# Hybrid decoder layer on one core: the feed-forward's down projection by one level of Strassen's form

## The chip, the cores and the metric

The kernel runs on one core of one Trainium2 chip. The metric is device time in microseconds (us) of one execution, the median of the runs shown; less is better. The matrix engine TensorE is called PE here, VectorE DVE, ScalarE ACT, GpSimd POOL, and the queue of SyncE, which issues all transfers named below, SP. L1056 is line 1056 of the kernel before, unless the text says that it is of the changed kernel.

## The reference

One layer for 2048 tokens of width 1024: a mixer (two groups of attention heads) with residual and LayerNorm, then a gated feed-forward network with a causal depthwise convolution of width 3 on the gate, again with residual and LayerNorm. The change lies in the feed-forward network alone:

```python
def conv_glu_ffn(h, w_ff_gate, w_ff_up, conv_w, conv_b, w_down):   # D_FF = 2816
    gate = h @ w_ff_gate
    up = h @ w_ff_up
    gp = jnp.pad(gate, ((0, 0), (CONV_WIDTH - 1, 0), (0, 0)))
    conv = sum(gp[:, i:i + S, :] * conv_w[i] for i in range(CONV_WIDTH)) + conv_b
    return (jax.nn.silu(conv) * up) @ w_down
# in the layer:
    y = conv_glu_ffn(h, ...)
    x = layer_norm(DEEPNORM_ALPHA * x + (1.0 + gate_f) * y, ln2_g[l], ln2_b[l])
```

## The kernel before

Everything is float32. A product is made of three passes of TensorE over operands that are split into a high and a low part (high by high, high by low, low by high). ACT makes the high part by a copy, DVE or POOL the low part by a subtraction; L101 is the line of a helper through which these urgent splits are issued, on each of the three engines.

**Gate and up.** The 2048 tokens are four tiles of 512, taken in two pairs, t2 = 0 and 1. The 22 blocks of 128 features are taken in 11 feature pairs, fp. For each t2 and fp there are two units, one for the gate and one for the up projection (unit, L1035). A unit makes two feature blocks for two token tiles by one level of Strassen's form: seven products of 12 matmuls of 128x512. For that the four quarters of the unit's weights are summed on DVE (tile wsum) and split (w_hi by ACT, w_lo by POOL for pieces of 128x1024, by DVE for those of 128x512). The sums of the token tiles are made once for each t2 (store_sums, L950; POOL's additions on tiles k, L958 to 961) and stored in DRAM. The first two feature pairs of the first two token tiles are done without Strassen's form (plain, L1108).

The gate unit's result goes through the convolution on DVE (conv_silu, L1103 to 1105) and SiLU on ACT (L1106) into a tile cv of 128x1024, one for each of the two feature blocks; there are two such buffers in all. The up unit multiplies its results into cv: put (L1051) adds the pieces on DVE into a small tile k (L1055; a ring of six buffers), POOL multiplies k into cv (L1056). Then cv is stored to the DRAM tensor da (L1090), and its buffer is free for the next pair's convolution.

**Down.** The activations (2048 x 2816) times w_down (2816 x 1024) are made in two halves of 512 output columns. Each half goes over 16 blocks of 128 tokens; a block is one accumulation over 22 feature blocks, three passes each (row_wide, L419 to 421). load_a (L1176) fetches a block's activations from da in three parts and splits them, in buffers that gate and up used before (pl, gt, wsum, cv in turn). The weights of the first half are loaded (L1162) and split while the last units run. In the first half the gated rows with their residual are stored to DRAM (dr0, L1224), in the second they come back (L1211), and DVE ends each block: gating, residual and statistics (L1217 to 1219), then the norm (L385 to 395), before the output is stored.

The order on each engine is set by a scheduler that simulates a timeline; what is issued through the urgent helper goes ahead of the rest. Each engine then runs its own list in order and waits at the head of it.

Of the kernel before, what the change touches and what calls it, by code (L numbers as in the profile page):

```python
# [27 lines left out]
P = 128  # L29
# [56 lines left out]
def layer(tc, x, c, w_ada, b_ada, w_in, gla_w_gate, gla_b_gate, sb_norm_g, gla_norm_g, w_out,  # L86
# [347 lines left out]
    da = [dram.tile([P, 2 * NB, NFF, P], F32, name=f"da{t}") for t in range(NT2)]  # L434
    dsum = {(t, i): [dram.tile([P, TQ], F32, name=f"dsum{t}{i}_{k}") for k in range(4)]
            for t in range(NT2) for i in (1, 3, 4, 6)}
    dr0 = [dram.tile([P, 512], F32, name=f"dr0_{b}") for b in range(NT * NB)]
# [400 lines left out]
    def run(gen):  # L838
        for _ in gen:
            pass  # L840
# [194 lines left out]
    def unit(n, order=range(7), after={}):  # L1035
# [25 lines left out]
        for i in order:  # L1061
# [35 lines left out]
            if i in after:  # L1097
                after[i]()

# [8 lines left out]
    def plain(t, x):  # L1108

        xh, xl = ([w[:, i, :] for half in x for w in half] for i in range(2))  # L1110
        for fp in range(CL):
            wg, wu = (weights(w[:, 256 * fp:256 * (fp + 1)], dve) for w in (w_ff_gate, w_ff_up))
            for j in range(2):
# [12 lines left out]
                nc.sync.dma_start(da[t // 2][:, t % 2 * NB:(t % 2 + 1) * NB, fb, :], cv.rearrange("p (b c) -> p b c", c=P))  # L1126
# [29 lines left out]

    slots = [(i, k) for i in range(7) for k in range(4)]

    def load_down(half, i, dst):

        raw = wring.tile([P, 1024], F32, name="w_raw", bufs=3)
        nc.sync.dma_start(raw.rearrange("p (k c) -> p k c", c=512),  # L1162
                          w_down[256 * i:256 * (i + 1), 512 * half:512 * (half + 1)].rearrange("(k p) c -> p k c", p=P))
        act.copy(dst[0], raw)
        dve.tensor_sub(dst[1], raw, dst[0])
        return [x.rearrange("p (k c) -> p k c", c=512) for x in dst]

    def t_pair(i):
        return [t_tile(*slots[2 * i + j]).rearrange("p k c -> p (k c)") for j in range(2)]

    wd = [[], []]
    for n in range(first, len(units)):
        unit(n, (0, 1, 3, 4, 2, 5, 6) if n == first else range(7))
    n_a = [0]

    def load_a(b):  # L1176

        hi, lo = [], []
        for f0 in range(0, NFF, 8):
            n = min(8, NFF - f0)  # L1180
# [4 lines left out]
            nc.sync.dma_start(w.bitcast(F32), da[b // (2 * NB)][:, b % (2 * NB), f0:f0 + n])  # L1185
# [6 lines left out]
    ahead = [load_a(0)]  # L1192
    wd[0] += [load_down(0, i, t_pair(i)) for i in range(NFF // 2)]
    gfb, g2b, b2b = rows = [t_tile(*slots[22 + i]).rearrange("p k c -> p (k c)").bitcast(F32) for i in range(3)]
    for d, src in zip(rows, (dgate[1], ln2_g, ln2_b)):
        nc.sync.dma_start(d, src.to_broadcast([P, D]))
    for half in range(2):
        ds = slice(half * 512, (half + 1) * 512)
        for b in range(NT * NB):
            xh, xl = ahead.pop()  # L1200
            if b + 1 < NT * NB or half == 0:
                ahead.append(load_a((b + 1) % (NT * NB)))
            ps = psm.tile([P, TQ], F32, name="acc", bufs=3)
            row_wide(ps, wd[half], xh, xl, slice(0, P))
            if half == 0 and b + 2 == NT * NB:
                wd[1] += [load_down(1, i, ring_pair()) for i in range(4)]
            if half == 0 and b + 1 == NT * NB:
                wd[1] += [load_down(1, i, t_pair(i - 4)) for i in range(4, NFF // 2)]
            if half:
                r = t_tile(*slots[25 + b % 2]).rearrange("p k c -> p (k c)").bitcast(F32)  # L1210
                nc.sync.dma_start(r[:, 0:512], dr0[b])  # L1211
                rh = r[:, 512:]
            else:
                rh = small()
            x1 = small()
            nc.sync.dma_start(x1, dx1[b // NB][b % NB][:, ds])
            nc.vector.tensor_mul(rh, ps, gfb[:, ds])  # L1217
            nc.vector.scalar_tensor_tensor(rh, x1, ALPHA, rh, ALU.mult, ALU.add)
            nc.vector.bn_stats(st_all[:, b, half, :], rh)
            if half:  # L1220
# [30 lines left out]
```

## Time and profile before

| | |
|---|---|
| runs | 2961.71, 2973.14, 2974.06 us; median 2973.14 |
| the profiled execution | 2961.73 us, of that 2960.0 us span |
| busy over the span | PE 94%, DVE 68%, ACT 37%, POOL 35% |
| second token pair's units, 2060 to 2437 us | PE busy in 373.49 of 377 us |
| down projection | first matmul at 2451.13 us, last at 2949.27 us |

The span is from the first to the last instruction. Matmuls overlap in the engine: one of 128x512 has a duration of 0.39 us in the rows, but the next starts 0.23 us after it. So PE's pace is read from the starts, and its losses from idle time before an instruction and from the granted clock, a share of full speed. The busy times of the other engines are sums of durations, and a duration includes what an operation waits while it runs.

### The profile page before, as it was taken

The numbers are of one execution on the slowest core, as the hardware profiler recorded it, in microseconds if no ns is written. First come the engines' busy times: TensorE is split into PE (matmuls) and PEld (weight loads), VectorE is DVE, ScalarE is ACT, GpSimd is POOL, SyncE is SP. The second block draws the span as 40 slices with busy tenths as digits, with TensorE's granted clock in tenths as the row PEclk, the third lists the DMA queues.
The fourth block names the chain that finished last, engine by engine and source line by source line (L and its number), as shares of the span: only waits on it lengthen the run. The fifth ranks groups of instructions, "written<-read, shape, count | busy, mean of one in ns | idle before, by whom it ended". The sixth has DMA issues, their size and how long they took to land. (4 is left out here: it accounts for less than half of the span.)

```text
span 2960.0 us, 38115 instructions
## 1 busy us (share of the span) xinstructions
PE 2773.9 (94%) x13387; PEld 2238.8 (76%) x13387; DVE 2018.8 (68%) x2841; ACT 1102.4 (37%) x1866; POOL 1035.4 (35%) x1139
## 2 busy tenths in 40 slices
PE   7989999999999998979879999989999998999998
PEld 6867887877788775657657787867888886888887
DVE  6474567578778779798667777686666765335665
ACT  2442244365557556534223332243232233112111
POOL 2450223246344345375463445462333440000000
PEclk9999999989999998989889999999999999999999
DMA  8977775766584445656785444354222236445553
GB/s 314 362 253 254 252 253 188 260 188 221 168 282 150 136 140 172 187 171 227 258 315 168 119 147 160 109 164 121 80 84 82 82 105 226 133 134 181 166 165 114
DMA packets 370424, 539.62 MB, mean 182 GB/s; under 512 B 25182, under 2 KB 224056, under 8 KB 370232
## 3 DMA queue, kind: packets, MB, share of 16 engines
q1 hardware_dynamic: 368504, 530.89, 55.6%
q0 software_dynamic: 1728, 6.29, 0.6%
q8 instruction: 106, 1.74, 0.2%
q14 instruction: 86, 0.70, 0.1%
HBM read 404.82 MB, written 132.26 MB: 181 GB/s over the span
## 5 line engine op out<-in xcount | busy, mean ns | idle before, releaser
L541 DVE TENSOR_TENSOR_SCAN pp<-pp,beta 128x512 f32<-128x512 f32 (+2 forms) x320 | 390.0, 1235 | 59.1 <-POOL beta L534 31.9
L543 POOL TENSOR_TENSOR beta<-beta,pp 128x512 f32<-128x512 f32 (+2 forms) x160 | 206.5, 1291 | 365.0 <-DVE pp L541 301.0
L101 POOL TENSOR_TENSOR w_lo<-wsum,w_hi 128x1024 fp32r<-128x1024 f32 x80 | 207.9, 2599 | 171.4 <-ACT w_hi L101 171.4
L1014 PE MATMUL acc<-t,w_lo 128*128 128x512 f32 x640 | 246.9, 392 | 9.2 <-DVE w_lo L101 9.2
L1012 PE MATMUL acc<-t,w_hi 128*128 128x512 f32 x640 | 250.4, 393 | 4.9 <-ACT k L1070 4.0
L1013 PE MATMUL acc<-t,w_hi 128*128 128x512 f32 x640 | 249.6, 390 | 0.0
L556 DVE TENSOR_TENSOR wl<-wt,wh 128x512 fp32r<-128x512 f32 (+1 forms) x320 | 185.2, 597 | 77.2 <-ACT wh L555 76.5
L555 ACT CAST wh<-wt 128x512 fp32r<-128x512 f32 (+1 forms) x320 | 161.0, 529 | 192.3 <-PE wt L551 182.7
L101 ACT CAST w_hi<-w_raw 128x512 fp32r<-128x512 f32 (+2 forms) x173 | 125.4, 746 | 253.1 <-PE acc L1013 64.8
L529 ACT ACTIVATE pp<-z 128x512 f32<-128x512 f32 (+2 forms) x320 | 173.5, 543 | 112.5 <-PE z L528 65.1
L292 PE MATMUL acc<-hh,w_hi 128*128 128x512 f32 x480 | 196.6, 411 | 3.2 <-DVE st L101 2.3
L551 PE MATMUL wt<-ident,beta 128*128 128x128 f32 x1088 | 189.6, 292 | 8.7 <-DVE beta L543 5.5
L294 PE MATMUL acc<-hh,w_lo 128*128 128x512 f32 x480 | 194.0, 405 | 0.6 <-POOL w_lo L101 0.6
L293 PE MATMUL acc<-hl,w_hi 128*128 128x512 f32 x480 | 192.4, 401 | 0.0
L101 DVE TENSOR_TENSOR w_lo<-w_raw,w_hi 128x512 fp32r<-128x512 f32 (+1 forms) x140 | 142.2, 1038 | 55.6 <-ACT w_hi L101 30.3
L530 ACT ACTIVATE beta<-z 128x512 f32<-128x512 f32 (+2 forms) x320 | 171.5, 542 | 18.4 <-PE wt L551 18.4
L551 PEld LDWEIGHTS wt<-ident,beta 128*128 128x128 f32 x1088 | 143.7, 150 | 41.8 <-DVE beta L543 7.9
L559 PE MATMUL o_ps<-wl,v 128*128 128x512 f32 (+1 forms) x320 | 133.9, 424 | 35.2 <-DVE wl L556 33.0
L527 PE MATMUL z<-k,q 128*128 128x512 f32 (+2 forms) x320 | 139.2, 439 | 11.4 <-ACT beta L530 8.6
L301 PE MATMUL acc<-w_hi,hh 128*128 128x256 f32 (+1 forms) x512 | 147.7, 289 | 1.4 <-ACT w_hi L101 0.7
L1014 PEld LDWEIGHTS acc<-t,w_lo 128*128 128x128 f32 x640 | 120.5, 188 | 37.4 <-DVE w_lo L101 12.2
L302 PE MATMUL acc<-w_lo,hh 128*128 128x256 f32 (+1 forms) x512 | 146.0, 286 | 0.9 <-POOL w_lo L101 0.9
(331 smaller groups left out, 7301.6 us busy)
## 6 DMA issues: line engine op xcount, KB each, us to landing
w_raw<-in_w_ff_gate_dram SPq DMA_DIRECT2D x48, 512.0 KB
w_raw<-in_w_ff_up_dram SPq DMA_DIRECT2D x48, 512.0 KB
k<-dk SPq DMA_DIRECT2D x160, 128.0 KB
v<-dv SPq DMA_DIRECT2D x80, 256.0 KB
da<-cv SPq DMA_DIRECT2D x40, 512.0 KB
w_hi<-dwi_0h SPq DMA_DIRECT2D x39, 512.0 KB
w_lo<-dwi_0l SPq DMA_DIRECT2D x39, 512.0 KB
q<-dq SPq DMA_DIRECT2D x128, 128.0 KB
```

Source lines behind the costliest of these rows:

```text
L101: return f(*args, **kw)
L292: nc.tensor.matmul(ps, hi[:, k % 4, cs], xh[k], start=(k == 0), stop=False)
L293: nc.tensor.matmul(ps, hi[:, k % 4, cs], xl[k], start=False, stop=False)
L294: nc.tensor.matmul(ps, lo[:, k % 4, cs], xh[k], start=False, stop=(k == nk - 1))
L529: nc.scalar.activation(pp[:, 0:n], z[:, 0:n], AF.Sigmoid, scale=-1.0)
L541: nc.vector.tensor_tensor_scan(pp[:, 0:n][:, ::-1], pp[:, 0:n][:, ::-1], beta[:, 0:n], first, ALU.mult, ALU.bypass)
L543: (nc.gpsimd if i in PMU and jt < PMJ else nc.vector).tensor_mul(beta[:, 0:n], beta[:, 0:n], pp[:, 1:n + 1])
L551: pe.transpose(wt[:, i * P:(i + 1) * P], ws[i][:, ks], ident)
L556: nc.vector.tensor_sub(wl[:, cs], wt[:, cs], wh[:, cs])
L1012: nc.tensor.matmul(ps, w[0][:, k, :], t[k][:, 0, :], start=first and k == 0, stop=False, **add)
L1013: nc.tensor.matmul(ps, w[0][:, k, :], t[k][:, 1, :], start=False, stop=False, **add)
L1014: nc.tensor.matmul(ps, w[1][:, k, :], t[k][:, 0, :], start=False, stop=k == 3, **add)
```

## The change

The down projection becomes seven products over pairs of token blocks (128 tokens each, 512 apart), pairs of feature blocks and the two halves of the output columns: 11 feature pairs by three passes for each product and each of eight block pairs. One product is taken for all eight pairs before the next. The quarters of w_down are summed on POOL (weight_sums, stored in dws), those of the activations too (act_sums, stored in dsa): in place on the cv tiles after each up unit, and on reloaded copies for the two feature pairs that plain made (plain_sums). The partial rows of all pairs stay on chip (top and low), and dr0 is gone. Weights go through a ring of 17 tiles, activations are loaded in two parts.

```diff
-                    nc.sync.dma_start(da[t2][:, :, 2 * fp + j, :], dst[j].rearrange("p (b c) -> p b c", c=P))
+                    nc.sync.dma_start(da[t2][:, :, j, fp], dst[j].rearrange("p (b c) -> p b c", c=P))
...
+        if up:
+            act_sums(t2, fp, dst[0][:, A], dst[1][:, A], dst[0][:, B], dst[1][:, B])
+
+    def act_sums(t2, fp, a11, a12, a21, a22):
+
+        nc.gpsimd.tensor_add(a22, a21, a22)
+        nc.gpsimd.tensor_sub(a21, a11, a21)
+        nc.gpsimd.tensor_sub(a11, a22, a11)
+        nc.gpsimd.tensor_sub(a12, a12, a11)
+        for j, x in enumerate((a22, a11, a21, a12)):
+            nc.sync.dma_start(dsa[t2][:, :, j, fp], x.rearrange("p (b c) -> p b c", c=P))
...
+    def weight_sums():
+
+        for k in range(NH):
+            for j, (m, n) in enumerate(((0, 0), (1, 0), (1, 1))):
+                nc.sync.dma_start(dws[k][4 + j], quarter(m, n, k))
+            b11, b12, b21, b22 = q = [small() for _ in range(4)]
+            for n, d in enumerate(q):
+                nc.sync.dma_start(d, quarter(n // 2, n % 2, k))
+            yield
+            nc.gpsimd.tensor_sub(b11, b12, b11)
+            nc.gpsimd.tensor_sub(b12, b22, b12)
+            nc.gpsimd.tensor_sub(b22, b22, b11)
+            nc.gpsimd.tensor_sub(b21, b21, b22)
+            for d, x in zip(dws[k], (b11, b12, b22, b21)):
+                nc.sync.dma_start(d, x)
+            yield
...
+    def plain_sums():
+
+        for fp in range(CL):
+            q = [small() for _ in range(4)]
+            for n, d in enumerate(q):
+                nc.sync.dma_start(d.rearrange("p (b c) -> p b c", c=P),
+                                  da[0][:, n // 2 * NB:(n // 2 + 1) * NB, n % 2, fp])
+            yield
+            act_sums(0, fp, *q)
+            yield
...
+    wsums = chain(plain_sums(), weight_sums())
+    for n in range(first, len(units)):
+        unit(n, (0, 1, 3, 4, 2, 5, 6) if n == first else range(7))
+        if n >= first + 4:
+            for _ in range(2):
+                next(wsums, None)
+    run(wsums)
...
+        for k in range(NH):
+            w = wset[i][k]
+            nc.tensor.matmul(ps, xh[k], w[:, 0, :], start=k == 0, stop=False)
+            nc.tensor.matmul(ps, xh[k], w[:, 1, :], start=False, stop=False)
+            nc.tensor.matmul(ps, xl[k], w[:, 0, :], start=False, stop=k == NH - 1)
...
+        if i == 0:
+            nc.scalar.copy(r[:, L], ps)
+        elif i == 1:
+            low.append(wide(NW + b))
+            nc.vector.tensor_add(low[b][:, L], r[:, L], ps)
+            nc.scalar.copy(r[:, R], low[b][:, L])
+            gated(r, blk, 0)
+        elif i == 2:
+            nc.vector.tensor_add(low[b][:, L], low[b][:, L], ps)
+        elif i == 3:
+            nc.vector.tensor_add(r[:, R], r[:, R], ps)
+            nc.vector.tensor_add(low[b][:, R], low[b][:, L], ps)
+            gated(low[b], blk + NB, 1)
+            stats(low[b], blk + NB, 1)
+            gated(low[b], blk + NB, 0)
+        elif i == 4:
+            finish(low[b], blk + NB, ps, False)
+        elif i == 5:
+            nc.vector.tensor_add(r[:, R], r[:, R], ps)
+            gated(r, blk, 1)
+            stats(r, blk, 1)
+        else:
+            finish(r, blk, ps, s + 1 == len(steps))
```

Two of the added functions in words: gated multiplies a half row by the gate and adds the residual (two operations of DVE); finish multiplies the product by the gate into a small tile, adds it to the row (L1266 and L1267 of the changed kernel), takes the statistics and runs the norm over the 1024 columns.

**The order on POOL, one feature pair of the second two token tiles.** Before, from the middle of an up unit into the next one: w_lo is the split of weight sums, cv the multiplication by the up results, gt a copy of two columns for the convolution.

```order
L101 TENSOR_TENSOR w_lo<-wsum,w_hi 128x1024
L1056 TENSOR_TENSOR cv<-cv,k_22173 128x512
L101 TENSOR_TENSOR w_lo<-wsum,w_hi 128x1024 x2
L1044 COPY gt<-halo 128x2 x2
L101 TENSOR_TENSOR w_lo<-wsum,w_hi 128x1024
L1056 TENSOR_TENSOR cv<-cv,k_22407 128x512
```

The same place in the changed kernel, with its own line numbers (L102 is the helper, L1057 the multiplication, L1105 to 1108 the four sums of activations, L1192 to 1195 the four sums of weights):

```order
L102 TENSOR_TENSOR w_lo<-wsum,w_hi 128x1024
L1057 TENSOR_TENSOR cv<-cv,k_22272 128x512
L1057 TENSOR_TENSOR cv<-cv,k_22295 128x512
L1192 TENSOR_TENSOR k_22310<-k_22311,k_22310 128x512
L1193 TENSOR_TENSOR k_22311<-k_22313,k_22311 128x512
L1194 TENSOR_TENSOR k_22313<-k_22313,k_22310 128x512
L1195 TENSOR_TENSOR k_22312<-k_22312,k_22313 128x512
L1105 TENSOR_TENSOR cv<-cv 128x512
L102 TENSOR_TENSOR w_lo<-wsum,w_hi 128x1024
L1106 TENSOR_TENSOR cv<-cv 128x512
L102 TENSOR_TENSOR w_lo<-wsum,w_hi 128x1024
L1192 TENSOR_TENSOR k_22468<-k_22469,k_22468 128x512
```

Between the last multiplication of a pair and the next split POOL now has four weight sums and one activation sum, and the other activation sums stand between the splits that the next gate unit waits for.

**The order on DVE, one block's end in the down projection.** Before, in the second half: a split of activations, the block's gating, residual and statistics, and the norm up to its first wide operation.

```order
L101 TENSOR_TENSOR pl<-pl 128x768
L1217 TENSOR_TENSOR t_2_25734<-acc,t_2_22778 128x512
L1218 SCALAR_TENSOR_TENSOR t_2_25734<-k_25736,t_2_25734 128x512
L1219 BN_STATS st<-t_2_25734 128x6
L385 BN_AGGR rn_mv<-st 128x2
L388 TENSOR_SCALAR rn_mv<-rn_mv 128x1
L394 SCALAR_TENSOR_TENSOR t_2_25734<-t_2_25734,rn_mv,t_3_22779 128x1024
```

In the changed kernel, at the begin of the fifth product:

```order
L102 TENSOR_TENSOR pl<-pl 128x768
L1266 TENSOR_TENSOR k_25017<-acc,t_1_23215 128x512
L102 TENSOR_TENSOR gt<-gt 128x640
L1261 BN_STATS st<-t_0_24078 128x6
L1267 TENSOR_TENSOR t_1_23677<-t_1_23677,k_25017 128x512
L102 TENSOR_TENSOR wsum<-wsum 128x768
L1261 BN_STATS st<-t_1_23677 128x6
L1266 TENSOR_TENSOR k_25086<-acc,t_1_23215 128x512
L386 BN_AGGR rn_mv<-st 128x2
L1267 TENSOR_TENSOR t_2_23732<-t_2_23732,k_25086 128x512
L389 TENSOR_SCALAR rn_mv<-rn_mv 128x1
L395 SCALAR_TENSOR_TENSOR t_1_23677<-t_1_23677,rn_mv,t_2_23216 128x1024
```

A block's end consists of the same kinds of operations, but it now comes after every 33 matmuls where it came after 66, and the ends of two blocks run into one another.

## Rows read from the trace of the kernel before

**Rows 1.** The page, the engines' busy time over the span, its share and the instructions.

```profile
PE 2773.9 (94%) x13387; PEld 2238.8 (76%) x13387; DVE 2018.8 (68%) x2841; ACT 1102.4 (37%) x1866; POOL 1035.4 (35%) x1139
```

**Rows 2.** Table by stretches. Columns: from:to, length, then busy time and instructions of PE, PEld (PE's weight loads), DVE, ACT and POOL, the granted clock, the share of the DMA engines and GB/s. In order: units of the first token pair; the same while store_sums(1) runs; units of the second token pair; the begin of the down projection; the rest of it.

```profile
1751.00:1811.00 60.00, 60.00 (x278) 49.71 (x277) 43.87 (x48) 22.61 (x29) 27.36 (x18) 1.00 0.44 135
1811.00:1869.00 58.00, 51.34 (x217) 41.21 (x216) 40.03 (x37) 14.75 (x20) 40.49 (x28) 0.94 0.63 199
2060.00:2437.00 377.00, 373.49 (x1642) 307.57 (x1642) 262.70 (x304) 114.17 (x150) 149.75 (x89) 1.00 0.29 86
2450.00:2490.00 40.00, 29.29 (x115) 22.71 (x114) 27.02 (x27) 17.41 (x17) 5.58 (x3) 0.83 0.88 306
2490.00:2950.00 460.00, 459.66 (x2028) 380.26 (x2027) 233.38 (x382) 94.19 (x96) 0.00 (x0) 1.00 0.48 150
```

**Rows 3.** Timeline of PE: start, duration, line and operation, and in brackets the idle time before it with what ended it. The first matmul of the down projection, two of its middle that are 14 matmuls apart, its last, and the two longest waits that the prediction speaks of.

```profile
1846.30 0.79 PE L1014 MATMUL acc<-t,w_lo 128*128 128x512 f32 x1 [4.41 <-DVE w_lo L101]
...
2451.13 0.39 PE L419 MATMUL acc<-t,pl 128*128 128x512 f32 x1
...
2482.92 0.80 PE L419 MATMUL acc<-t,cv 128*128 128x512 f32 x1 [9.57 <-ACT cv L101]
...
2599.76 0.39 PE L421 MATMUL acc<-t,gt 128*128 128x512 f32 x1
...
2602.93 0.39 PE L420 MATMUL acc<-t,wsum 128*128 128x512 f32 x1
...
2949.27 0.39 PE L421 MATMUL acc<-t,cv 128*128 128x512 f32 x1
```

**Rows 4.** Timelines of POOL and DVE at places in the gate and up units: start, duration, engine, line and operation. The first is a sum of store_sums(1), the others are of the second token pair.

```profile
1811.32 1.29 POOL L958 TENSOR_TENSOR k<-k,k 128x512 f32<-128x512 f32 x1 [1.13 <-DMA k<-dh]
...
2276.33 2.66 POOL L101 TENSOR_TENSOR w_lo<-wsum,w_hi 128x1024 fp32r<-128x1024 f32 x1 [4.85 <-ACT w_hi L101]
2285.38 2.85 POOL L101 TENSOR_TENSOR w_lo<-wsum,w_hi 128x1024 fp32r<-128x1024 f32 x1 [6.39 <-ACT w_hi L101]
...
2278.32 0.69 DVE L1058 TENSOR_TENSOR gt<-k,acc 128x512 f32<-128x512 f32 x1 [0.98 <-PE acc L1014]
...
2286.01 3.31 DVE L1104 SCALAR_TENSOR_TENSOR cv<-gt,ccols,cv 128x1024 f32<-128x1024 f32 x1
...
2294.10 1.27 DVE L1104 SCALAR_TENSOR_TENSOR cv<-gt,ccols,cv 128x1024 f32<-128x1024 f32 x1
```

**Rows 5.** Groups of instructions of POOL and of DVE between 2060 and 2437 us, of those whose operands all lie in SBUF: line, engine, operation, shapes and count, busy time, mean ns of one, and the idle time before them with what ended it.

```profile
L101 POOL TENSOR_TENSOR w_lo<-wsum,w_hi 128x1024 fp32r<-128x1024 f32 x39 | 100.0, 2565 | 122.1 <-ACT w_hi L101 122.1
L1056 POOL TENSOR_TENSOR cv<-cv,k 128x512 f32<-128x512 f32 x30 | 43.2, 1442 | 38.2 <-DVE k L1055 31.7 <-ACT cv L1106 6.4
...
L101 DVE TENSOR_TENSOR w_lo<-w_raw,w_hi 128x512 fp32r<-128x512 f32 x59 | 51.3, 897 | 22.6 <-PE acc L1014 22.6
L1104 DVE SCALAR_TENSOR_TENSOR cv<-gt,ccols,cv 128x1024 f32<-128x1024 f32 x19 | 42.5, 2238 | 0.5
L101 DVE TENSOR_TENSOR wsum<-w_raw 128x512 f32<-128x512 f32 x39 | 37.0, 950 | 34.0 <-POOL w_lo L101 20.7 <-DMA w_raw<-in_w_ff_up_dram 7.9 <-DMA w_raw<-in_w_ff_gate_dram 5.5
L1105 DVE SCALAR_TENSOR_TENSOR cv<-gt,ccols,cv 128x1024 f32<-128x1024 f32 x19 | 26.4, 1390 | 0.2
L1103 DVE TENSOR_SCALAR cv<-gt,ccols 128x1024 f32<-128x1024 f32 x19 | 14.2, 749 | 0.8
L101 DVE TENSOR_TENSOR wsum<-wsum,w_raw 128x512 f32<-128x512 f32 x19 | 14.1, 743 | 0.7
...
L101 DVE TENSOR_TENSOR wsum<-w_raw,wsum 128x512 f32<-128x512 f32 x20 | 13.7, 683 | 0.0
```

**Rows 6.** Groups of POOL between 1811 and 1869 us, one of the four additions of store_sums(1); columns as above.

```profile
L961 POOL TENSOR_TENSOR k<-k,k 128x512 f32<-128x512 f32 x4 | 6.8, 1694 | 0.2
```

**Rows 7.** The chain that ended last (what each thing waited for, followed back), at two places: a load around 2040 us, and the begin of the down projection. Columns: start, duration, what.

```profile
2040.27 3.64 DMA t<-dh
...
2461.66 2.21 POOL cv L1056
...
2463.89 10.83 DMA da<-cv
...
2474.79 6.89 DMA cv<-da
...
2481.83 1.05 ACT cv L101
```

**Rows 8.** Timeline of DVE, one block's end in the second half of the down projection; between the rows shown lie L1218 and L1219 of 0.69 us each and small operations.

```profile
2800.93 0.96 DVE L101 TENSOR_TENSOR pl<-pl 128x768 fp32r<-128x768 f32 x1 [4.50 <-ACT pl L101]
2801.81 0.68 DVE L1217 TENSOR_TENSOR t<-acc,t 128x512 f32<-128x512 f32 x1
...
2805.55 1.22 DVE L101 TENSOR_TENSOR gt<-gt 128x1024 fp32r<-128x1024 f32 x1
...
2808.44 1.28 DVE L395 SCALAR_TENSOR_TENSOR t<-t,rn_rs,t 128x1024 f32<-128x1024 f32 x1
2809.96 1.23 DVE L101 TENSOR_TENSOR wsum<-wsum 128x1024 fp32r<-128x1024 f32 x1 [0.23 <-ACT wsum L101]
```

**Rows 9.** The chain that ended last, the end of the kernel; columns as in Rows 7.

```profile
2949.70 0.70 DVE t L1217
...
2956.21 0.66 DVEq L1247
```

More of the change, by code (lines that the diff above doesn't have):

```diff
@@ L1154, in layer @@
     run(sets_of(1, (2, 5)))
+    NP2 = NT * NB // 2
+    NH = NFF // 2
+    NW = 17
+    PARTS = ((0, 6), (6, NH - 6))
     slots = [(i, k) for i in range(7) for k in range(4)]
[L1159 to L1176, printed above, removed]
+    wide = lambda n: t_tile(*slots[n]).rearrange("p k c -> p (k c)").bitcast(F32)
+    dws = [[dram.tile([P, 512], F32, name=f"dws{k}_{j}") for j in range(7)] for k in range(NH)]
+    def quarter(i, j, k):
+        return w_down[(2 * k + i) * P:(2 * k + i + 1) * P, 512 * j:512 * (j + 1)]
@@ L1178, in load_a @@
+    def load_a(i, b):
         hi, lo = [], []
-        for f0 in range(0, NFF, 8):
-            n = min(8, NFF - f0)
+        src = products[i][1](b)
+        for f0, n in PARTS:
             pool, name = ((ft, "pl"), (right["ft2"], "gt"), (ft, "wsum"), (right["ft2"], "cv"))[n_a[0] % 4]
@@ L1184, in load_a @@
                     for _ in range(2))
-            nc.sync.dma_start(w.bitcast(F32), da[b // (2 * NB)][:, b % (2 * NB), f0:f0 + n])
+            nc.sync.dma_start(w.bitcast(F32), src[:, f0:f0 + n])
             act.copy(h, w.bitcast(F32))
@@ L1190, in load_a, with gated @@
         return hi, lo
-    ahead = [load_a(0)]
-    wd[0] += [load_down(0, i, t_pair(i)) for i in range(NFF // 2)]
-    gfb, g2b, b2b = rows = [t_tile(*slots[22 + i]).rearrange("p k c -> p (k c)").bitcast(F32) for i in range(3)]
+    def gated(r, blk, half):
+        ds = slice(half * 512, (half + 1) * 512)
+        x1 = small()
+        nc.sync.dma_start(x1, dx1[blk // NB][blk % NB][:, ds])
+        nc.vector.tensor_mul(r[:, ds], r[:, ds], gfb[:, ds])
+        nc.vector.scalar_tensor_tensor(r[:, ds], x1, ALPHA, r[:, ds], ALU.mult, ALU.add)
@@ L1195, in layer @@
+    for n in range(first, len(units)):
[4 more added lines that the diff above has]
+    run(wsums)
+    steps = [(i, b) for i in range(7) for b in range(NP2)]
+    ahead = [load_a(0, 0)]
+    wset = [[load_w(0, k) for k in range(NH)]] + [[] for _ in range(7)]
+    gfb, g2b, b2b = rows = [wide(25 + i) for i in range(3)]
     for d, src in zip(rows, (dgate[1], ln2_g, ln2_b)):
         nc.sync.dma_start(d, src.to_broadcast([P, D]))
[L1197 to L1220, printed above, removed]
-                dst = out[b * P:(b + 1) * P, :]
-                norm(r, st_all[:, b], g2b, b2b, nc.vector, m1, (dst[:, 0:512], dst[:, 512:D]) if b == NT * NB - 1 else (dst,))
-            else:
-                nc.sync.dma_start(dr0[b], rh)
@@ new lines, in layer @@
+    top = [w.bitcast(F32) for _ in range(NP2 // 2) for w in ring_pair()]
+    low = []
+    L, R = slice(0, 512), slice(512, D)
+    for s, (i, b) in enumerate(steps):
+        xh, xl = ahead.pop()
+        if s + 1 < len(steps):
+            ahead.append(load_a(*steps[s + 1]))
+        ps = psm.tile([P, TQ], F32, name="acc", bufs=3)
+        for k in range(NH):
[3 more added lines that the diff above has]
+            nc.tensor.matmul(ps, xl[k], w[:, 0, :], start=False, stop=k == NH - 1)
+        if i < 6:
+            if 0 < b < NW - NH + 1:
+                wset[i + 1].append(load_w(i + 1, b - 1))
+            elif b == NP2 - 1:
+                wset[i + 1] += [load_w(i + 1, k) for k in range(NW - NH, NH)]
+        r, blk = top[b], b // NB * 2 * NB + b % NB
+        if i == 0:
[21 more added lines that the diff above has]
+            finish(r, blk, ps, s + 1 == len(steps))
```

35 lines of the change are left out of this document (32 added, 3 removed).

## The prediction, made before the changed kernel was run

> **What bounds the kernel now.** I began with the page: PE is busy in 94% of the span, DVE in 68%, POOL in 35% [rows 1]. Such means hide that each stage has its own limit, so I took a table by stretches next [rows 2]. In the down projection behind 2490 us PE is busy in 459.66 of 460 us at full clock; only its begin, 2450 to 2490, has 29.29 of 40 us at a clock of 0.83. The units of the second token pair have 373.49 of 377 us. So PE's list sets the time nearly everywhere, and what matters is how far the other engines are from stopping it. One stretch shows them close: from 1811 to 1869 POOL also makes the 16 additions of store_sums(1); it is busy in 40.49 of 58 us, and PE in only 51.34, at a clock of 0.94, where the minute before had 60.00 of 60.
>
> PE's pace is read from starts [rows 3]: 14 matmuls lie between 2599.76 and 2602.93, 0.2265 us each. The 2112 matmuls of the down projection take 498.1 us; at 0.227 they would take 479.4, so 19 us are lost, nearly all at the begin.
>
> Then I looked why POOL's additions stop PE. POOL and DVE wait for one another [rows 4]: L1104 on DVE takes 1.27 us alone and 3.31 where POOL's w_lo runs from 2285.38 to 2288.23; it ends one microsecond behind that. An operation of DVE that reads PSUM (L1058, 0.69 us within the w_lo of 2276.33) doesn't wait. So the busy times of the two must be added, for operations whose operands all lie in SBUF. The groups between 2060 and 2437 us give the sum [rows 5]: POOL has 100.0 + 43.2 = 143.2 us. DVE has 137 operations of 128x512 at 0.683 (93.6), 38 of 128x1024 at 1.27 (48.3) and L1103 with 14.2: 156.1 us. A feature pair lasts 38.6 us there (168 matmuls by 0.227 are 38.1, and 3.5 us in ten pairs are idle), so of 9.77 pairs one takes 14.7 us on POOL and 16.0 on DVE, 30.7 of 38.1 us together.
>
> **The change, part by part.** The sum is made against the profiled execution, 2961.73 us, which is 11.4 us below the median of the runs.
>
> *Fewer matmuls.* 7 x 8 x 11 x 3 = 1848 stand in the place of 2112, of the same shape: 264 x 0.227 = -59.9 us. PE being the bound of this stage, that comes off the path.
>
> *Sums of weights.* 11 blocks of four POOL operations, and two blocks for plain_sums, are spread by two steps behind each unit over 13 units, 6.5 feature pairs. With the activation sums of the same pairs POOL has 12 more operations of 128x512 for each pair, at 1.29 us without a wait [rows 4] 15.5 us: 30.7 + 15.5 = 46.2 us of work that excludes itself, in 38.1 us of PE. It no longer fits. The nearest rows are those of store_sums(1), the same four operations, 1.69 us each when DVE is in the way [rows 6]: 51.34 us at a clock of 0.94 are 48.3 us of full work in 58 us, or 1.27 pairs, so a pair lasts 45.8 us, with 16 / 1.27 = 12.6 additions in it. PE's longest wait there is 4.41 us for a w_lo [rows 3]. That measured period and the sum of 46.2 agree. Against 38.6 before it is 7.2 us for a pair; I take 7.4, since the cv buffers are also held longer, and 6.5 pairs give **+48 us**. Bounds: nothing, if all of it falls into POOL's idle time, and 12 x 1.29 x 6.5 = 101 if nothing is hidden.
>
> *Sums of activations elsewhere.* 13.5 pairs get four operations each, 5.2 us: 30.7 + 5.2 = 35.9 of 38.1 fits, barely. About 1.5 of these pairs lie under store_sums(1), where nothing is left: 6 operations at the precedent's price ((58 - 48.3) / 16 = 0.6 us each) are 4. For the other 12 I take 0.6 us a pair, a quarter of that price: 7. **+11**, bounds 0 and 54 x 0.6 = 32. Each sum's four stores are new issues on SP; they stand behind a wait for POOL, and the weight loads of the units stand behind them. SP's issue is hidden as long as two transfers of 3.64 us (the load of rows 7) lie within a unit of 19 us.
>
> *Begin of the down projection.* Before, PE waits 9.57 us for the first block's part in cv [rows 3]: the last multiplication, the store of cv (10.83 us at 0.88 of the DMA engines' time), the load (6.89), the split [rows 7]. After, the first accumulation has 11 feature pairs in pl and gt alone, and PE's list puts work of later pairs ahead of what waits. But the last pair's sums and their stores come behind the store of cv, and are first needed by the second product 60 us later. **-9 us**; bounds -14 (the whole loss up to 2490) and +10 (one more such landing).
>
> *Ends of blocks.* PE takes 33 x 0.227 = 7.49 us for one accumulation. DVE's end of a block lasts from 2801.81 to 2809.72, 7.9 us with one split of 1.22 in it [rows 8]. Without that split and with the two of 768 and 640 columns (0.96 and some 0.8) it is 8.5, in the fifth product with 0.68 more for a weight split. The sixth product needs some 5 us of DVE and takes up what the fifth leaves; the eight accumulations of the last product end with up to 8 x 1.0 us of DVE's work left, of which I take **+6** (bounds 0 and 18). The last block's own 6.5 us [rows 9] are the same in both. Products 1 to 4 need less, and dr0's stores and loads vanish from a stage in which DMA was at 0.48: nothing either way, since PE waits for none of them; should a load be late there, a block of 7.49 us is its cover.
>
> Sum: -59.9 + 48 + 11 - 9 + 6 = **-4 us**, 2957.8 by the profiled execution's time. Since that execution stands 11.4 below the median, I add half of it: **2964 us**.
>
> **The rivals.**
>
> *The sums are hidden.* By share of time POOL has 149.75 us of 377 [rows 2], 40%, and 15.5 us in 38.1 bring it to 80%; DVE stays at 70%. If idle time is what counts, the stretch costs nothing, nor do the other sums, and -59.9 - 9 + 6 and 4 for the pairs under store_sums(1) are -59: 2903, or 2908 with the half difference. For it speaks that weight pieces are made three ahead and that the scheduler places the sums. Against it speaks the same four operations' price at 1811 us. The Trainium skill (Perfetto Trace Analysis, Identifying the Most-Contended Engine) says that for Vector, Scalar and GPSIMD the occupancy is a fair measure of how close an engine is to its roofline; by that, neither engine would be at its limit and this case would be the likeliest. The trace does not agree: at 40.49 of 58 us, 70%, POOL already stopped PE. But a part of the stretch may fit, the scheduler having put the sums elsewhere than there: 28%.
>
> *The cv buffers are held too long.* This one ends slower. The sums are made in place: they start when cv's store has landed, and the buffer is free only when their own stores have. From the last up product: L1055 0.7, L1056 1.3, a transfer of 3.64, four operations 5.2, another 3.64: 14.5 us. The next pair's convolution wants the buffer after six of seven products, 16.3 us. So it decides from landings of 4.5 us on average; the store at 2463.89 took 10.83. With landings of 6 and operations at 1.5 us the chain takes 20 us, and PE is held by some 3 us in each of the 13.5 pairs outside the stretch as well: +40, 3003. For it: the added DMA traffic of every pair; against it: a DMA share of only 0.29 between 2060 and 2437. 22%.
>
> *DVE bounds the last three products.* If splits and finishes don't overlap as they do now, each of 24 accumulations lasts 9 us for 7.49: +36 for +6, so some 2994. Against it: DVE's 233.38 of 460 us now. 8%.
>
> **How the numbers follow.** The forecast has 42%; its own range, with 6 to 9 us for a pair and the bounds of the smaller terms in part, is 2938 to 2990. A measurement of this kernel tells some 0.5%, 15 us, from no change, so the bounds lie at 2958 and 2988. Of the forecast's 42% I put 9 under, 30 within and 3 over; of the hidden sums' 28%, 27 under; of the held buffers' 22%, 21 over; of DVE's 8%, 3 within and 5 over. Together: faster 0.36, same 0.35, slower 0.29. The range is 2908 to 3010: under it lies half of the hidden sums' case, over it the worst of the held buffers'.
>
> **What would show it.** In the table by stretches of the changed kernel: 6.5 pairs of the second token pair at some 45 to 46 us for 168 matmuls, with a lower granted clock, PE's idle time in them ended by w_lo or wsum, and POOL over 30 us busy in 40. In the other pairs less than a microsecond more than before. A begin of the down projection with no wait near 9.57. 1848 matmuls from first to last in some 425 to 435 us. The end after the last matmul under 15 us. I am wrong if the pairs with weight sums stay near 39 to 41 us, or if PE's idle time ends with the convolution (L1103 of before) waiting for a transfer.

## The result

The changed kernel takes 3001.55 us in the median (2990.16 to 3002.38, four runs) where the kernel before takes 2969.39 on the same chip: a ratio of 1.0102, with an interval from 1.0072 to 1.0131. It is 1.0% **slower**. The prediction said 2964 and no change that can be told; 3001.55 lies within its range of 2908 to 3010, but 38 us above its forecast, and the whole interval lies above 1.

The profiled execution of the changed kernel has a span of 2988.2 us, 28.2 more than that of before. Both profiled executions are the fastest of their runs, so the traces show 28.2 us of the 32.2 between the medians. The page of the changed kernel gives the engines' busy times, to be set against [rows 1], and two rows of slices (40 slices of some 75 us; tenths of a slice that PE was busy, tenths of full clock that it was granted):

```profile
PE 2739.0 (92%) x13123; PEld 2201.7 (74%) x13123; DVE 2105.4 (70%) x2984; ACT 1127.8 (38%) x1953; POOL 1220.1 (41%) x1271
...
PE   6889999998999998989889999989988989899998
...
PEclk8989999999999999989889999999999999999999
```

The same two rows of the page of the kernel before:

```profile
PE   7989999999999998979879999989999998999998
PEclk9999999989999998989889999999999999999999
```

PE has 264 matmuls less, and POOL 185 us more work than in [rows 1]. But the very first slices are the surprise: PE at 6, 8, 8 tenths where it was at 7, 9, 8, with the clock down to 0.8 in the first and third, in a part of the program whose code the change did not touch.

To see where the time went, take the starts of the matmuls at the same places of both traces. PE's timeline of the changed kernel at the first gate unit, at the 1597th matmul of the units (19 units of 84 matmuls lie before it, one of them of the second token pair, and all of plain), and at the first and last matmul of the down projection (start, duration, line, operation):

```profile
1620.12 0.39 PE L1013 MATMUL acc<-t,w_hi 128*128 128x512 f32 x1
...
2082.23 0.39 PE L1013 MATMUL z<-t,w_hi 128*128 128x512 f32 x1
...
2537.35 0.39 PE L1296 MATMUL acc<-t,pl 128*128 128x512 f32 x1
...
2976.33 0.39 PE L1298 MATMUL acc<-t,cv 128*128 128x512 f32 x1
```

and of the kernel before at the two places that [rows 3] lack:

```profile
1596.47 0.39 PE L1012 MATMUL acc<-t,w_hi 128*128 128x512 f32 x1
...
2051.66 0.39 PE L1014 MATMUL wt<-t,w_lo 128*128 128x512 f32 x1
```

| stage | before, us | after, us | change | the prediction's terms |
|---|---|---|---|---|
| up to the first gate unit | 1596.5 | 1620.1 | **+23.7** | none |
| first token pair's units, plain, the second pair's first unit | 455.2 | 462.1 | +6.9 | activation sums, +11 in all |
| second token pair's other 21 units | 399.5 | 455.1 | +55.6 | weight sums +48, and the rest of the 11 |
| down projection, first to last matmul | 498.1 | 439.0 | -59.2 | -59.9 - 9 |
| after the last matmul | 10.8 | 11.8 | +1.1 | +6 |

The five add up to the 28.2 but for rounding. The last four rows make +4.4 where the sum said -4; the first row is missing in it altogether. Below, "the second token pair's units" are the 21 of the third row.

**What stands in the first row.** SP's transfers of the changed kernel that write the tensor of weight sums, over the whole run (line, transfer, count; least, median and longest duration of the issue in ns; first and last start in us):

```profile
L1187 SPq DMA_DIRECT2D dws<-in_w_down_dram x33: 490/586/1346, 31.7 to 76.6; - x33
...
L1197 SPq DMA_DIRECT2D dws<-k x44: 319/327/840, 2211.6 to 2453.6; - x44
```

weight_sums issues three copies from DRAM to DRAM for each feature pair, of the three quarters of w_down that three of the seven products take as they are. In the code they stand inside a block of the second token pair, as do the stores of L1197, which run there. But a copy reads an input and waits for nothing, so the scheduler listed all 33 at the begin. The table by stretches, 40 to 80 us (columns as in [rows 2]), of the kernel before:

```profile
40.00:80.00 40.00, 33.05 (x183) 28.64 (x183) 20.95 (x30) 12.38 (x19) 14.04 (x7) 0.91 0.86 312
```

and of the changed kernel:

```profile
40.00:80.00 40.00, 27.35 (x121) 22.74 (x120) 13.71 (x26) 7.39 (x12) 7.10 (x4) 0.74 1.04 370
```

The DMA engines, at 0.86 of their time before, are now full (1.04); PE gets 121 matmuls done for 183, at a clock of 0.74.

### The profile page after: what moved, and what is told of

It reads as the page before. It is cut to its first block, busy times and chain, and to the rows that moved or that the text cites. A ratio compares the mean times of both kernels' runs of the same rounds, so it can differ in the third digit from the quotient of the medians.

```text
span 2988.2 us, 38718 instructions
## 1 busy us (share of the span) xinstructions
PE 2739.0 (92%) x13123; PEld 2201.7 (74%) x13123; DVE 2105.4 (70%) x2984; ACT 1127.8 (38%) x1953; POOL 1220.1 (41%) x1271
## 5 line engine op out<-in xcount | busy, mean ns | idle before, releaser
L542 DVE TENSOR_TENSOR_SCAN pp<-pp,beta 128x512 f32<-128x512 f32 (+2 forms) x320 | 389.9, 1233 | 60.7 <-POOL beta L535 32.2
L102 ACT CAST w_hi<-w_raw 128x512 fp32r<-128x512 f32 (+2 forms) x169 | 121.2, 740 | 301.7 <-PE acc L1014 130.3
L102 POOL TENSOR_TENSOR w_lo<-wsum,w_hi 128x1024 fp32r<-128x1024 f32 x80 | 205.2, 2565 | 27.8 <-ACT w_hi L102 26.2
L552 PEld LDWEIGHTS wt<-ident,beta 128*128 128x128 f32 x1088 | 143.0, 149 | 39.9 <-issue 6.6
L533 POOL TENSOR_SCALAR_AFFINE_SELECT pp<-pp 128x128 f32<-128x128 f32 x128 | 61.7, 483 | 250.2 <-ACT pp L530 244.6
L1013 PE MATMUL wt<-t,w_hi 128*128 128x512 f32 x320 | 132.0, 413 | 34.5 <-DVE k L1081 34.0
L102 DVE TENSOR_TENSOR wsum<-w_raw 128x512 f32<-128x512 f32 x80 | 101.2, 1267 | 72.5 <-POOL w_lo L102 53.8
```

The source lines that it names most:

```text
L102: return f(*args, **kw)
L542: nc.vector.tensor_tensor_scan(pp[:, 0:n][:, ::-1], pp[:, 0:n][:, ::-1], beta[:, 0:n], first, ALU.mult, ALU.bypass)
L552: pe.transpose(wt[:, i * P:(i + 1) * P], ws[i][:, ks], ident)
L1013: nc.tensor.matmul(ps, w[0][:, k, :], t[k][:, 0, :], start=first and k == 0, stop=False, **add)
```

## The experiments

Theory A: the 33 copies make the first row. Theory B is the prediction's own for the second token pair: operations of POOL and DVE on SBUF exclude one another, and their sum of 46.2 us for a feature pair sets its length. Its rival, H: the blocks wait for their transfers, and hold small tiles and cv buffers meanwhile.

### The copies alone, added to the kernel before (e1)

```diff
+    dws = [[dram.tile([P, 512], F32, name=f"dws{k}_{j}") for j in range(3)] for k in range(NFF // 2)]
     for n in range(first, len(units)):
         unit(n, (0, 1, 3, 4, 2, 5, 6) if n == first else range(7))
+        k = n - first - 6
+        if 0 <= k < NFF // 2:
+            for j, (a, b) in enumerate(((0, 0), (1, 0), (1, 1))):
+                nc.sync.dma_start(dws[k][j], w_down[(2 * k + a) * P:(2 * k + a + 1) * P, 512 * b:512 * (b + 1)])
```

> The kernel before, with nothing changed but 33 copies of quarters of w_down from DRAM to DRAM (256 KB each), as the changed kernel has them; nothing reads the copies. They wait for nothing, so the scheduler puts them early on SP. Theory A: the changed kernel's first 165 us lost some 18 us, and 24 us by the first gate unit, because these copies (8.65 MB read, 8.65 MB written) run where the DMA engines are full. Then this kernel's first gate unit starts 18 to 26 us later than before's 1596 us, nothing else moves, and the whole is about 2985 to 2992 us by 2969. Rival: the begin differs because the whole program was listed anew, or from run to run; then the first unit starts within 4 us of 1596 and the time stays near 2969.

Measured: 2991.22 us for 2968.71, ratio 1.0069 (1.0043 to 1.0095), 22.5 us more. The copies are issued from 31.6 to 77.2 us, and the first gate unit starts at 1622.8, 26.3 later than before. The stretch from 40 to 80 us looks as in the changed kernel:

```profile
40.00:80.00 40.00, 26.32 (x114) 21.50 (x114) 13.64 (x26) 7.44 (x11) 7.10 (x4) 0.74 1.03 359
```

The rest stays: 400.2 us for the second token pair's units, 499.2 for the down projection. Theory A holds with all else as before.

### The changed kernel without the copies (e2)

```diff
-            for j, (m, n) in enumerate(((0, 0), (1, 0), (1, 1))):
-                nc.sync.dma_start(dws[k][4 + j], quarter(m, n, k))
...
-    products = [(lambda k: dws[k][4], partial(act_quarter, 0, 0)),
+    products = [(partial(quarter, 0, 0), partial(act_quarter, 0, 0)),
...
         raw = w[:, 1, :].bitcast(F32)
+        if isinstance(products[i][0], partial):
+            raw = wring.tile([P, 1024], F32, name="w_raw", bufs=3)[:, 0:512]
```

> The changed kernel without the 33 copies: the three products that take a plain quarter of w_down load it from w_down itself through a raw tile. Theory A: the first gate unit starts within 4 us of before's 1596 us, and the whole falls by 20 to 26 us, to about 2976 to 2981. Rival (the new listing costs the begin): within 5 us of 3001. The pairs with weight sums stay at 45 to 46 us by both.

Measured: 2972.86 us, ratio to before 1.0013 (0.9995 to 1.0032): 28.7 us less than the changed kernel. The first gate unit starts at 1604.0, and from 40 to 80 us PE has its matmuls again:

```profile
40.00:80.00 40.00, 33.85 (x186) 29.32 (x186) 20.79 (x30) 12.75 (x20) 14.38 (x7) 0.87 0.87 316
```

The first gate unit starts some 7.5 us later than before, where up to 4 were expected; of the 19.8 us between the two spans 16.1 lie ahead of it, and 4.2 in the down projection, which now loads these quarters through a raw tile. Without the copies the change is what the prediction's sum said, none that can be told; the single terms of that sum come further down.

### The copies kept, but late (e9)

```diff
+                nc.sync.dma_start(dws[k][4 + j][0:1, 0:P], da[1][0:1, 0, 0, done[0], :])
                 nc.sync.dma_start(dws[k][4 + j], quarter(m, n, k))
...
+        done[0] = units[n][1] - 1 + units[n][2]
```

> The changed kernel with its 33 copies kept, but each held back: a row of 512 bytes of da is first stored into the copy's target, so the copy can start only when a feature pair of the second token pair is done. Theory A: the copies cost only where the DMA engines are full. The first gate unit starts at 1596 to 1609 us in the place of 1620, the second token pair's units (DMA share 0.54 there) stay within 5 us of 455, whole 2970 to 2982. Rival: 17 MB of traffic cost the same wherever they run, or SP's list, which now waits for the small stores, pays it back in the units: whole above 2990.

Measured: 2977.01 us, ratio 1.0022 (1.0004 to 1.0039); the copies run from 2172.2 to 2412.6 us, the first gate unit starts at 1589.9, the second token pair's units take 455.5 us for 455.1. Among these units, where the DMA share is 0.67 with the copies, the same 33 copies cost 4 us by the medians of this kernel and e2, which has none, a difference that the two intervals do not separate. It is the place that costs, and little of it the traffic.

### Weight sums left out (e3), and their additions alone (e5)

For e3, on the kernel of e2:

```diff
-                (lambda k: dws[k][2], partial(act_sum, 1)),
+                (partial(quarter, 1, 0), partial(act_sum, 1)),
...
-    wsums = chain(plain_sums(), weight_sums())
+    wsums = plain_sums()
```

> As the one with direct loads, and the weight sums are left out: no loads, additions and stores for them, the products take plain quarters of w_down in their place (so the result is not the layer's); plain_sums and the activation sums stay. Theory B: the pairs of the second token pair are at 45 us for 38.6 because the additions of POOL exclude DVE; without the 8 of the weights, 30.7 + 5.2 = 35.9 us fit and the pairs fall to 38.5 to 39.5: 6.5 pairs by 6 to 7 us, about 40 to 45 us off the second token pair's units, whole about 2935 to 2940. Rival: the activation sums alone, which hold the cv buffers, make the pairs long; then they stay above 42 us and the gain is under 20 us.

For e5, on the kernel of e3:

```diff
+    def additions():
+        x, y = (tsets[1, 0][i][:, 0, :].bitcast(F32) for i in range(2))
+        for k in range(NH):
+            yield
+            for _ in range(4):
+                nc.gpsimd.tensor_sub(small(), x, y)
+            yield
-    wsums = plain_sums()
+    wsums = chain(plain_sums(), additions())
```

> As the one without weight sums, with POOL's 44 additions of 128x512 put back where the weight blocks had them, but on data that lie on chip, out into the ring of small tiles: no loads, no stores, nothing reads the results (the products take plain quarters, so the result is not the layer's). Theory B (work of POOL and DVE that excludes itself, 46.2 us a pair): the pairs with additions go back to 44 to 46 us and the whole to about 2962 to 2970. Rival H (blocks wait for transfers: loads, stores that must land before a small tile or a cv buffer is free): additions alone cost little, the pairs stay under 41 us, the whole under 2940. In between, both have a part.

Measured: e3 2923.63 us, ratio 0.9854 (0.9809 to 0.9898); e5 2962.78, ratio 0.9986 (0.9973 to 0.9999). The second token pair's units take 452.4 us in e2, 405.1 in e3, 438.3 in e5. Weight sums thus cost 47.3 us there. 33.2 of them come with POOL's additions alone, without any transfer of the weight sums; 14 come with the loads, stores and held tiles. Theory B has the larger part, H the smaller. Six pairs of e2, that is 1008 matmuls of the units from start to start (table by stretches):

```profile
2190.30:2468.20 277.90, 243.66 (x1010) 198.14 (x1009) 199.45 (x186) 68.92 (x90) 198.48 (x125) 0.93 0.55 176
```

The same six of e3 (the first still has a block of plain_sums):

```profile
2184.90:2417.10 232.20, 229.21 (x1009) 188.94 (x1008) 174.50 (x187) 67.72 (x90) 128.22 (x82) 1.00 0.39 111
```

and of e5:

```profile
2186.30:2448.20 261.90, 239.22 (x1010) 192.66 (x1009) 196.90 (x186) 68.63 (x90) 194.41 (x123) 0.97 0.34 97
```

In e2 POOL and DVE are each busy in 71 to 72% of the stretch, and PE stands for 34 us at a clock of 0.93. In e3's pairs without any block a unit takes 19.04 us, which is PE's pace: the activation sums alone cost nothing there. That operations wait for one another shows in the durations: DVE has 187 operations and 174.50 us in e3, 186 and 196.90 in e5, 22 us of the 30 by which the six pairs are longer. One rival is not separated by any run: POOL works through its list in order, so in e5 the additions also delay the w_lo and the activation sums behind them, whether or not they exclude DVE.

The wait that H speaks of can be seen in the changed kernel, in the chain that ended last around 2400 us (start, duration, what):

```profile
2398.00 1.71 POOL cv L1107
...
2399.73 4.60 DMA dsa<-cv
...
2404.46 1.81 DVE cv L1115
...
2410.63 0.61 DVE k L1081
```

and in PE's timeline behind it:

```profile
2411.28 0.79 PE L1013 MATMUL wt<-t,w_hi 128*128 128x512 f32 x1 [6.88 <-DVE k L1081]
```

An activation sum takes 1.71 us, beside an operation of DVE, for 1.29 without; its store takes 4.60 us to land; the convolution waits for the cv buffer; and L1081, which PE waits for, stands behind the convolution in DVE's list. Over six pairs of the changed kernel, 2204 to 2484 us, PE is idle for 35.0 us, and most of that ends with L1081 (group of PE: shapes and count, busy us, mean ns, idle us before with what ended it):

```profile
L1013 PE MATMUL wt<-t,w_hi 128*128 128x512 f32 x96 | 42.8, 446 | 29.3 <-DVE k L1081 29.3
```

But the buffer is the smaller part of these waits. DVE's timeline ahead of the one above:

```profile
2398.47 1.78 DVE L102 TENSOR_TENSOR wsum<-w_raw 128x512 f32<-128x512 f32 x1
...
2404.46 1.80 DVE L1115 TENSOR_SCALAR cv<-gt,ccols 128x1024 f32<-128x1024 f32 x1 [1.89 <-POOL k L1194]
```

In the five waits that end with L1081, of 3.8 to 6.9 us, DVE is itself idle before the convolution for only 1.5 to 1.9 us. For the rest it works, on operations that take long beside POOL's: 1.78 us for a wsum that takes 0.68 alone, 1.80 for an L1115 of 0.75. In e5 PE's idle time of 22.7 us ends for 20.3 with w_lo, on DVE (14.7) or POOL.

### One block a pair for two (e6)

weight_sums comes first here and plain_sums last, so that blocks can begin in the first token pair:

```diff
         for _ in range(3):
             next(cols_todo, None)
+        if n >= first - 6:
+            next(wsums, None)
...
-        if n >= first + 4:
-            for _ in range(2):
-                next(wsums, None)
+        next(wsums, None)
```

> As the one with direct loads, with one weight block in a feature pair in the place of two, from the twelfth unit of the first token pair on. Theory B: a pair needs 30.7 + 5.2 + 5.2 = 41.1 us of work that excludes itself, so all 11 pairs of the second token pair take about 41.5; that stage gains only what its empty pairs had to spare, some 15 us, whole 2955 to 2962. Rival H: with half as many blocks nothing waits for a small tile, the pairs fall to 38.5 to 39.5, whole 2930 to 2938.

Measured: 2974.66 us, ratio 1.0027 (1.0007 to 1.0047): no gain. A pair takes 42.9 us, and there are twice as many of them; H as the main cause falls. It missed what theory B said for the whole too: the second token pair's units fell by 6 us for 15, to 446.0, and the first token pair's, among whose last the blocks now begin, rose by 14 over e2's.

### The additions on DVE: weight sums (e4), all sums (e7)

e4 puts the four operations of weight_sums on nc.vector in the place of nc.gpsimd, e7 those of act_sums too.

> As the one with direct loads, and the four additions of each weight block are on DVE in the place of POOL. Theory B (work that excludes itself): an addition of 128x512 takes 0.68 us on DVE for 1.29 on POOL, so the sum of a pair falls from 46.2 to 41.3 us and the pairs from 45.4 to about 41.5: some 25 us off, whole about 2952 to 2957. Rival (POOL's list, the waits for transfers at its head, and the held cv buffers make the pairs long): DVE then waits for the loads at its own head, and the pairs stay at 45 or more.

> As the one with the weight sums on DVE, and the four activation sums on DVE too. Theory B: 30.7 + 12 x 0.68 = 38.9 us of work that excludes itself, but DVE alone has some 27 + 8.2 = 35 of 38.1 us and waits at the head of its list for stores of cv to land; pairs at 41 to 43 for 43.9, whole 2945 to 2955. Rival H: DVE now waits for the landing of cv's store with the convolution behind it, the pairs get longer than 45 us, whole above 2965.

Measured: e4 2957.61 us, ratio 0.9968 (0.9948 to 0.9988), a pair 44.8 us: 15 us gained where theory B said 25, the pair well above its 41.5 and near the rival's 45. But DVE's own waits for the block's loads come to 1.5 us over six pairs. PE's idle time, 27.4 us in six waits, ends each time with a w_lo of DVE, and each time additions of a block ran on DVE within the 16 us before, one or two of them taking 1.8 to 2.9 us for 0.68, and DVE had no gap over 0.3 us. By that, it is DVE's own list that got too long here. e7: 2944.98 us, ratio 0.9919 (0.9888 to 0.9950), a pair 41.2 us, as expected; H's rival, pairs above 45, did not come.

### The weight sums in the down projection (e8)

```diff
+        t = wring.tile([P, 1024], F32, name="w_raw", bufs=3)
+        for n, q in enumerate(pair):
+            nc.sync.dma_start(t[:, 512 * n:512 * (n + 1)], quarter(*q, k))
...
+    dst = x[0][0]
+    nc.gpsimd.tensor_sub(dst, *x[0])
```

> As the one with direct loads, and the weight sums are made in the down projection itself, where POOL has nothing to do: each weight tile's quarters are loaded, added on POOL (7 additions for each of 11 feature pairs over four products) and split, with no stores. By both theories the second token pair's units fall by 45 to 49 us, as without weight sums. Down projection: 77 x 1.29 = 99 us of POOL beside 240 us of PE, where DVE is at 50 to 70%: 0 to 10 us more. Whole 2920 to 2935, faster than the kernel before by 1 to 1.6%. It fails if three raw tiles are too few to bring the loads ahead: then PE waits in products 1, 2 and 4.

Measured: 2963.19 us, ratio 0.9981 (0.9963 to 0.9999). The second token pair's units fell to 405.5 us as expected, but the down projection went from 434.8 to 477.3. What each engine waited for between 2530 and 2800 us (engine, tile, line, cause; us in all, times, longest):

```profile
POOL w_raw L1214 <- DMA w_raw<-in_w_down_dram: 109.6, 24, 38.8
...
ACT t L102 <- POOL w_raw L1214: 23.5, 11, 4.5
```

It failed much in the way named: POOL waits for loads into the raw tiles, and ACT, whose list also holds the splits of the activations, waits behind POOL. PE's waits behind the begin end with splits, of activations more than of weights, and with an operation of DVE (6.3 us). Whether more raw tiles would mend it, no run shows.

### Half density with the sums on DVE: weight sums (e10), all sums (e11), other parts (e12)

All three have e2's direct loads and one step of the blocks, two of which make a block, behind each unit of the second token pair but the first; the last two blocks come behind the units. e12 also has PARTS = ((0, 8), (8, NH - 8)).

```diff
-        if n >= first + 4:
-            for _ in range(2):
-                next(wsums, None)
+        if n > first:
+            next(wsums, None)
```

> Weight sums on DVE, activation sums on POOL, direct loads, and one weight block for each feature pair of the second token pair (the last two blocks behind the units). Theory B by its sum: 30.7 + 5.2 + 2.7 = 38.6 us a pair, at the edge; since the pairs so far took 0 to 3.5 us more than the sum where it was above 38.1, 38.5 to 41: the stage's 442 us become 410 to 430, whole 2925 to 2945. If one block at a time still stops PE by its waits for transfers, the pairs stay above 42.

> As the one before, and the activation sums on DVE too. Theory B by its sum: 30.7 + 8 x 0.68 = 36.1 us a pair, under 38.1: the pairs at 38.1 to 39.5, the stage at 402 to 412 us for 424 with two blocks a pair, whole 2922 to 2935, 1.2 to 1.6% faster than the kernel before. Rival: DVE's list, which waits for cv's store to land in every pair, costs 2 us a pair whatever the density; then the stage stays above 418 and the whole above 2938.

> As the one before, with a block's activations loaded in parts of 8 and 3 feature pairs in the place of 6 and 5. The begin of the down projection waits 7 to 8 us for the part that holds the last feature pair; with 8 feature pairs in each first part PE has 48 matmuls of two first parts, 10.9 us, where it had 36, 8.2 us: the wait falls by some 2.7 us, the whole by 0 to 4 us. If the longer splits of 1024 columns hold up other work in the down projection, it loses as much.

Measured: e10 2945.28 us, ratio 0.9925 (0.9900 to 0.9950), stage 421.8 us. **e11 2924.47 us, ratio 0.9860 (0.9835 to 0.9885)**, stage 411.7 us: the fastest kernel here but for e3, which leaves the weight sums out: 1.4% faster than before and 2.6% faster than the change by the medians. A pair takes 40.9 us in e10 and 39.9 in e11, where up to 39.5 was expected. Six pairs of e11:

```profile
2184.70:2423.90 239.20, 233.46 (x1009) 190.95 (x1008) 203.14 (x235) 68.57 (x90) 88.62 (x55) 0.99 0.52 158
```

DVE is busier than in e2, 85%, POOL at 37%, and PE stands for 6 us in place of 34. e12: 2930.76 us, ratio 0.9879 (0.9854 to 0.9903). The longest wait at the begin of the down projection is 11.8 us where e11 has 8.1, and it is another part that ends it, the third block pair's first one (pl) in place of its second (gt). The guess was wrong, and so was its picture of that wait, as the next section shows.

## Why the prediction was wrong

**The failed step: the weight sums' copies.** Against a sum of -4 us the traces show +28.2. Of the 32 us between them 24 are the first row, which the sum does not have; 10 are the begin of the down projection; the units are 3.5 over and the ends of blocks 5 under. The prediction's step on the weight sums counts "12 more operations of 128x512" for a pair and the waits on POOL and DVE. Of each block's seven loads and copies it says nothing, so they were costed at nothing, with no work named that hides them. Four of them run where the code has them; the three copies were listed at 31.7 us, into a stretch where the DMA engines, at 0.86 before, had little time left. By the medians, adding them to the kernel before costs 22.5 us, taking them out of the change gives 28.7, and moving them gives 24.5. The prediction argues from POOL's, DVE's and PE's lists, and of SP's only with the stores of the sums. The rival that would have ended slower, cv buffers held too long, was the wrong one: pairs outside the stretch run at PE's pace.

How much of the first row is the copies stays open to some 10 us by the traces, one execution each. In the twelve kernels without early copies the first gate unit started between 1589.9 and 1611.6 us, with nothing changed in that part but the listing; with them it started at 1620.1 and 1622.8. The medians above are the firmer measure.

**Weight sums, +48: the size right, the mechanism in the main, and some luck.** 47.3 were measured as the difference of e2 and e3. The prediction put all of it down to work that excludes itself; 33.2 come with the additions alone, and the other 14 come with the blocks' transfers, which it had at nothing. That the two add up to its 48 is luck. Nor did PE's idle time end as it said, with w_lo or wsum: 29.3 of 35.0 us ended behind the convolution, which the prediction named as a sign of being wrong. The sign came, but at most 2 us of each of these waits goes back to DVE's wait for the buffer, and the rest is DVE at work beside POOL.

The sum of excluded work is a guide to some 3 us, not a law: pairs measured 46.3 us by a sum of 46.2 (e2), 38.1 by 35.9 (e3's plain pairs), but 44.8 by 41.3 (e4), 42.9 by 41.1 (e6), 41.2 by 38.9 (e7), 40.9 by 38.6 (e10), 39.9 by 36.1 (e11). What adds the 0 to 3.5 us over the larger of the sum and 38.1 is not shown in general; e5, without transfers of the weight sums, lies 2.5 below its sum, at 43.7.

**Activation sums, +11: size nearly right, place wrong.** The second token pair's pairs without a block cost nothing, where I had 0.6 us each. The first token pair's 18 units take 9.8 us more, 7.6 of it in the last one, 28.4 us for 20.7. No run leaves the activation sums out; e1, which has none, has 2.5 us more in the same 18 units.

**The sums hidden (a rival): it was not so.** In e2 POOL is busy in 198.48 and DVE in 199.45 of 277.90 us, and the pairs are 8 us too long. The Trainium skill (Perfetto Trace Analysis, Identifying the Most-Contended Engine) takes an engine's occupancy as a fair measure of its closeness to the limit; the trace does not agree for these two, which are busy in 71 and 72% of the stretch and yet hold PE up: without the weight sums (e3) as many matmuls take 232.20 us.

**Begin of the down projection, -9: wrong.** One wait of [rows 3] went, and another came. The prediction misread the old one: the part in cv was not the first block's, whose 66 matmuls were done by then, but the second block's first, with tokens of the first token pair: its load needed nothing of the last feature pair but the cv buffer. The new wait is for the second part of the third block pair, in gt. The chain, and PE's timeline, of the changed kernel:

```profile
2557.12 8.11 DMA gt<-da
```

```profile
2566.09 0.80 PE L1296 MATMUL acc<-t,gt 128*128 128x512 f32 x1 [7.50 <-ACT gt L102]
```

The first to last matmul takes 19.5 us more than 1848 x 0.227 in the changed kernel and 15.3 in e2, for 18.7 before: nothing was gained, or 3.4 us in e2. I had seen that PE's list puts other work ahead, and not that this work is short: 27 matmuls, 6.1 us, stand between the two uses of the gt buffers, for a load of 8.11 us. That load was moreover issued only at 2557.12, behind the last store into da (2556.43) in SP's list, 5.0 us after the last matmul on the part before had started. Which of the two counts for more, no run separates.

**Fewer matmuls, -59.9: right**; 264 matmuls less, at the same pace. **Ends of blocks, +6: too much**, 1.1 measured after the last matmul. The rival of DVE bounding the last products did not come either: from 2580 us on PE is busy in 394.42 of 397 us.

## What to carry to other kernels

Look in the changed list of every queue, transfers above all, for where an added instruction really stands: here one that waits for nothing was listed at the begin, not where the code has it, and a full stretch paid for it. Where two engines exclude each other, add their work up before you add more to either, and put an addition on the one that does it faster. Taking out the copies turned a loss of 1.0% into no change (e2), and the same sums on DVE at half the density turned that into a gain of 1.4% (e11). An engine that is busy 70% of the time can still hold up the others.

## What was not expected of the hardware

The same 33 copies of 256 KB cost 22 to 29 us at the begin, where the DMA engines were at 0.86 without them, and some 4 us at 2172 to 2412 us, where they were at 0.67 with them. And moving additions from POOL to DVE made the kernel faster, though DVE was the busier of the two over the span [rows 1]: an addition of 128x512 takes 0.68 us on DVE and 1.29 to 1.75 on POOL, and DVE's 235 operations in six pairs of e11 take 203 us where 186 took 199 in e2.
